# Reordering the first three weight blocks of a hybrid SSM/convolution layer: product 6 ahead of product 7, a table setup that starts later, and its small copies on VectorE

## The chip, the cores and the metric

The kernel runs on one core of a Trainium2 chip. The metric is the device time of one execution in microseconds (us). The kernel before takes 1282.01 us, the median of three runs (1280.66, 1282.01 and 1284.53).

The core has a matrix engine (TensorE, PE in the profile), VectorE (DVE), ScalarE (ACT), GpSimd (POOL) and SyncE (SP), which here only issues DMAs. Each engine works off its own list of instructions in the order in which the program wrote them; semaphores make it wait for another engine's result.

## The reference, cut to what matters

```python
proj = x @ w_in + b_in                         # x: 1024 x 1024, w_in: 1024 x 4096
u, h, c_gate, b_gate, gate_a, gate_b = split(proj)
y_a = s5_ssm(u, lambda, log_dt, B, C, D)       # complex diagonal scan, 32 groups of 64 states
g   = gelu(y_a)
y_a = (g * sigmoid(g @ glu_w + glu_b)) @ w_ssm_out
y_b = (b_gate * causal_conv(c_gate * h)) @ w_conv_out
mix = (sigmoid(gate_a) * y_a + sigmoid(gate_b) * y_b) @ w_o
x   = layer_norm(alpha * x + mix)
x   = layer_norm(alpha * x + (silu(x @ w_gate) * (x @ w_up)) @ w_down)
```

All of it is in float32. The part that the change touches is the first projection (blocks of `w_in`), the constants of the scan, which are worked out on the chip from `lambda` and `log_dt`, and the order of the first blocks of `w_gate` and `w_up`.

## The kernel before, in words

**Products.** A pair of weight columns blocks times the 1024 tokens is a 2 x 2 by 2 x 2 block product, done in seven products in Strassen's way. `WOP` (L152) and `XOP` (L154) say which sum or difference of blocks each of the seven products m = 1 to 7 takes on the weight side and on the x side. Each operand of a product is split into a high and a low float32r part ("lo" and "hi"): ScalarE writes the rounded high part (L121, or L137 and L138 when the rounded copy also goes to a PSUM tile `hp`), VectorE subtracts it from the operand (L115). A product is then 12 matmuls of 128x512: four slices k of the contraction, each lo·hi, hi·lo and hi·hi (L183 to L185). In the first stage the products 2 and 5 of the first three pairs skip the split and use unsplit float32 operands (L179).

**PSUM banks.** `BANK_OF` (L157) puts products 2 and 4 of a pair in its bank 0, 5 and 3 in bank 1, 1 and 7 in bank 2, 6 in bank 3. Product 7 is accumulated on top of product 1, so it can only start after ScalarE has copied product 1 out of the bank (the tile `ec`, or `z` for the second pair, L237). A bank of a later product takes the PSUM buffer of an earlier one: six buffers go round in order of allocation. `Pair.ev` (L207 to L263) is run after each product and issues the combinations: copies `ea`, `eb`, `ec` on ScalarE, `ea+eb` and `ec-ea` on GpSimd (L239, L241), `b0-ea`, `b1+ec` and the last additions on VectorE (L253, L255, L257, L259), then the epilogue of the block.

**Steps.** A step is one product of one pair. `LEAD` (L305, L306) is the order of the first 21 steps: three pairs interleaved, first products 2, 4, 5, 3 of each, then 1, 7, 6 of pairs 0 and 1, then 1, 7, 6 of pair 2. In the first projection the pairs are u0, u2 and gt0 (tiles `_u`, `_u`, `_gt`); in the gated feed-forward stage they are f0, f1, f2 (`_f`). `run` (L325) issues the instructions of step s in this order: its own loads, the weight sum of step s+4 (GpSimd, tile `t`, or `ws` for the unsplit products), the weight split of step s+3 (ScalarE and VectorE, tiles `wh` and `wl`), one turn of each background generator that is due, the matmuls of step s, epilogues that are due, the `mid` work, and then `Pair.ev`.

**The x operands.** `make_x` (L432) makes the x operands of the first stage in `mid` of steps 0 to 19: for products 4, 3, 1, 7, 6 a sum on GpSimd in four slices (tile `xs`, L449) and two slices later the split (tiles `xh`, `xl`); for 5 and 2 the split alone. The sums use two tiles in turn.

**The setup of the SSM branch.** `setup` (L497) is a generator that works out the tables `E`, `Lim`, `nLre`, `Mre`, `sMim` and `ph8` from the parameters. It is a chain of small VectorE operations, 128x32 to 128x288, in 22 pieces (each ends at a `yield`), with two Sin activations on ScalarE. Pieces 1 to 11 are issued ahead of step 0 (L1349, L1375, L1379, L1387); from step 0 on one piece is issued per step, ahead of the matmuls of the step (L1391): 12 at step 0, 13 at step 1, the Sin piece 16 at step 4, the piece that writes `Mre` at step 10, the piece that writes `sMim` at step 13. After that it idles until step 21, closes its scratch and starts the branch's own generators. `Mre` and `sMim` are each written by eight small instructions on GpSimd, one per power j (L627, L634).

**The feed-forward stage.** The same `LEAD` orders the first 21 steps there. The third pair's banks 0 and 1 are copied out early to tiles `keep` (L242 to L247), which the first projection doesn't do.

Of the kernel before, what the change touches and what calls it, by code (L numbers as in the profile page):

```python
# [47 lines left out]
def kernel(  # L48
# [22 lines left out]
    V, S, G, PE = nc.vector, nc.scalar, nc.gpsimd, nc.tensor  # L71
# [27 lines left out]
    sgn = const.tile([P, 3], F32, tag="sgn", name="sgn")  # L99
# [5 lines left out]
    def tt(o, a, b, op, eng=V):  # L105
        eng.tensor_tensor(o, a, b, op)  # L106
# [10 lines left out]
    def ts(o, a, s1, s2, op0, op1, eng=V):  # L117
        eng.tensor_scalar(o, a, s1, s2, op0, op1)  # L118
# [184 lines left out]
    steps = []  # L303
    ORD_A = (2, 5, 1, 4, 3, 7, 6)
    LEAD = [(i, m) for m in (2, 4, 5, 3) for i in (0, 1, 2)]  # L305
    LEAD += [(i, m) for m in (1, 7, 6) for i in (0, 1)] + [(2, 1), (2, 7), (2, 6)]  # L306

    def add_pairs(pairs, lead, nl):
        for i, m in lead:
            steps.append(pairs[i].step(m))  # L310
        for p in pairs[nl:]:
            base = len(steps)
            for m in ORD_A:
                steps.append(p.step(m))
            for i, back in ((1, 7), (0, 6)):
                steps[base - back].pre.append(lambda p=p, i=i: p.load(i))
# [27 lines left out]
    def start(gen, s=0):  # L344
        bg.append([gen, s])
# [63 lines left out]
    def mkpair(f0, f1, nm, ep, f):  # L409
        p = Pair(w1[f0], w1[f1], nm, xcombo, ep)  # L410
        p.f = f
        return p

    gp_ = [mkpair(16 + d, 24 + d, f"gt{d}", epi_g, d) for d in range(8)]
    pairs = [mkpair(0, 1, "u0", epi_u, 0), mkpair(2, 3, "u2", epi_u, 2), gp_.pop(0)]
# [16 lines left out]
    def make_x():  # L432
        waiting = []

        def low(h, l, k, src):
            (psplit if k % 2 else split)(h[:, k], l[:, k], src)

        for n, m in enumerate((4, 3, 1, 7, 6, 5, 2)):
            op = XOP[m]
            if len(op) == 3:  # L440
                sums = xcp.tile([P, 4, 512], F32, tag=("xh2", "xl2")[n % 2], name=f"xs{m}")
            h = xh[m] = xcp.tile([P, 4, 512], F32R, tag=f"xh{m}", name=f"xh{m}")
            l = xl[m] = xcp.tile([P, 4, 512], F32R, tag=f"xl{m}", name=f"xl{m}")
            for k in range(4):
                if len(op) == 1:
                    src = xr[op[0]][:, k]
                else:
                    src = sums[:, k]
                    tt(src, xr[op[1]][:, k], xr[op[2]][:, k], OPS[op[0]], G)  # L449
                waiting.append((h, l, k, src))  # L450
                if len(waiting) > 2:
                    low(*waiting.pop(0))
                yield 1
        for w in waiting:
            low(*w)
            yield 1
# [17 lines left out]
    for p in pairs[:3]:  # L474
        p.drops = {4: 1}
        p.whole = {2: wsum, 5: wsum}
    add_pairs(pairs, LEAD, 3)
    for n, i, q in ((1, 1, 0), (3, 0, 1), (5, 1, 1)):
        steps[n].pre.append(lambda i=i, q=q: pairs[i].load(q))
    steps[7].pre.append(lambda: load_f(pairs[2], 1))  # L480
# [16 lines left out]
    def setup():  # L497
# [3 lines left out]
        Mre = tb["Mre"] = pre.tile([P, NG, 8], F32, tag="Mre", name="Mre")  # L501
        sMim = tb["sMim"] = pre.tile([P, NG, 8], F32, tag="sMim", name="sMim")
# [8 lines left out]
        def carve(*shape, at=None):  # L511
            n = int(np.prod(shape))
            o = used[0] if at is None else at
            if at is None:
                used[0] += n
            t = scr[:, o : o + n]
            return t.rearrange("p (a b) -> p a b", a=shape[0]) if len(shape) == 2 else t
# [11 lines left out]
        m, r, q = carve(NG), carve(NG), carve(NG)  # L529
# [92 lines left out]
        x8, y8 = t9[:, :, 0:8], u9[:, :, 0:8]  # L622
# [1 line left out]
        mul(y8, Lim[:, :, 0:8], fib)  # L624
        sub(x8, x8, y8)
        for j in range(8):
            G.tensor_copy(Mre[:, :, j], x8[:, :, 7 - j])  # L627
        yield 1
        mul(x8, nLre[:, :, 0:8], fib)
        mul(y8, Lim[:, :, 0:8], frb)  # L630
        add(x8, x8, y8)
        yield 2
        for j in range(8):
            G.tensor_scalar_mul(sMim[:, :, j], x8[:, :, 7 - j], sgn[:, 0:1])  # L634
        ts(nLre, nLre, sgn[:, 0:1], -1.0, ALU.mult, ALU.mult)
        while psum_state["n"] > 4 or next(xg, None):
            yield 1
# [604 lines left out]
    fps = []  # L1242
# [7 lines left out]
    fps[2].kept = lambda i: cst_["zp"].tile([P, 512], F32, tag=f"keep{i}", name=f"keep{i}")  # L1250
    for p in fps[:3]:
        p.drops = {4: 1}
    add_pairs(fps, LEAD, 3)
    n_end = len(steps)
    def begin_d0():
        flush()
# [89 lines left out]
    ramp = tb["ramp"] = pre.tile([P, P], F32, tag="ramp", name="ramp")  # L1346
    dss = tb["dss"] = pre.tile([16, NG], F32, tag="dss", name="dss")
    early_setup = setup()
    next(early_setup)  # L1349
    raw = pairs[0].raw[1] = wring.tile([P, KT, P], F32, tag="raw", name="raw_u0_1", bufs=4)  # L1350
# [32 lines left out]
    steps[2].add()  # L1383
    steps[2].split()
    steps[3].add()
    for _ in range(4):
        next(early_setup)  # L1387
    xg = make_x()
    for n, cnt in enumerate((2, 2, 2, 1, 2, 1, 2, 1, 2, 1, 2, 1, 2, 2, 1, 2, 1, 1, 1, 1)):
        steps[n].mid.append(lambda cnt=cnt: [next(xg, None) for _ in range(cnt)])  # L1390
    start(early_setup)  # L1391

    def spin():
        for it in list(bg):
# [143 lines left out]
    for n in range(len(seq)):  # L1538
        m, kp = seq[n]
# [156 lines left out]
```

## Time and profile before

| what | value |
|---|---|
| median of three runs | 1282.01 us (1280.66 to 1284.53) |
| profiled execution, its own time | 1284.58 us |
| profiled execution, span from first to last instruction | 1282.8 us |
| granted TensorE clock, mean | 0.979 |
| TensorE busy | 1208.3 us, 94% of the span |
| VectorE busy | 830.6 us, 65% |
| GpSimd busy | 792.8 us, 62% |
| ScalarE busy | 763.8 us, 60% |

In a row of the timeline the columns are: start in us, duration in us, engine, line, operation, output<-inputs, shape, number of instructions merged into the row, and in square brackets the idle time before it on its engine and what ended it. In the table of waits a row reads: engine, tile and line of the waiting instruction, what it waited for, us in total, number of waits, the longest. In the table by stretches each engine's busy us stands with its number of instructions, in the order PE, PE weight loads, DVE, ACT, POOL, then the granted clock, the DMA share and GB/s.

### The profile page before, as it was taken

To read this page: it belongs to the slowest core of one execution; us is meant where nothing else is said; L and a number is where in the kernel's file an instruction comes from. 1 tells how busy PE (TensorE), PEld (TensorE's weight loads), DVE (VectorE), ACT (ScalarE), POOL (GpSimd) and SP (SyncE) were. 2 spreads that over 40 slices of the span, in tenths; PEclk is the share of its full clock that TensorE was granted. 3 is DMA by queue.
4 is the path that set the end of the run, shared out by engine and by line. 5 is a ranking of instruction groups with operands and counts; after the bars stand their busy time and mean duration, and the time that the engine had idled before them with its cause. 6 is when DMAs were issued, how large, how long until landed. Compare 5 with 4: busy or idle time off the path is not lost. (4 is left out here: it accounts for less than half of the span.)

```text
span 1282.8 us, 16767 instructions
## 1 busy us (share of the span) xinstructions
PE 1208.3 (94%) x5341; PEld 977.2 (76%) x5341; DVE 830.6 (65%) x1322; ACT 763.8 (60%) x1359; POOL 792.8 (62%) x609
## 2 busy tenths in 40 slices
PE   4968999999998999999988999999999999999996
PEld 1646787777777888888866888888888887888776
DVE  8784787979754757588875444434444437667777
ACT  2765777787886424133574555545555545778891
POOL 4575888788753213322488877787787774544466
PEclk8988999999999999999989999999999999999999
DMA  7213244344357535323502533232233426936312
GB/s 252 66 66 99 66 125 120 103 143 138 112 161 224 188 123 183 128 89 116 173 33 94 177 108 114 93 123 99 83 115 107 140 91 247 379 98 214 106 43 90
DMA packets 88455, 167.63 MB, mean 131 GB/s; under 512 B 17840, under 2 KB 27056, under 8 KB 88112
## 3 DMA queue, kind: packets, MB, share of 16 engines
q1 hardware_dynamic: 87760, 166.44, 38.9%
q8 instruction: 42, 0.69, 0.2%
q14 instruction: 45, 0.37, 0.1%
q10 hardware_dynamic: 608, 0.13, 0.1%
HBM read 116.34 MB, written 44.83 MB: 126 GB/s over the span
## 5 line engine op out<-in xcount | busy, mean ns | idle before, releaser
L183 PE MATMUL ps_f<-x1h,wl_f 128*128 128x512 f32 x616 | 242.1, 393 | 8.4 <-ACT keep L246 2.3
L184 PE MATMUL ps_f<-x1l,wh_f 128*128 128x512 f32 x616 | 240.9, 391 | 0.6 <-DVE x1l L115 0.6
L185 PE MATMUL ps_f<-x1h,wh_f 128*128 128x512 f32 x616 | 241.1, 391 | 0.0
L115 DVE TENSOR_TENSOR wl_f<-t_f,hp 128x512 fp32r<-128x512 f32 x107 | 73.5, 687 | 168.9 <-ACT hp L137 168.6
L137 ACT ACTIVATE hp<-t_f 128x512 fp32r<-128x512 f32 x107 | 64.4, 602 | 175.8 <-POOL t_f L106 169.3
L183 PEld LDWEIGHTS ps_f<-x1h,wl_f 128*128 128x128 f32 x616 | 116.4, 189 | 35.4 <-ACT keep L246 2.7
L184 PEld LDWEIGHTS ps_f<-x1l,wh_f 128*128 128x128 f32 x616 | 116.5, 189 | 24.8 <-DVE x1l L115 1.0
L185 PEld LDWEIGHTS ps_f<-x1h,wh_f 128*128 128x128 f32 x616 | 116.3, 189 | 24.4
L106 POOL TENSOR_TENSOR tB<-B,B 128x512 f32<-128x512 f32 x55 | 71.3, 1297 | 84.1 <-DVE rBl L115 45.3
L1517 PE MATMUL pe<-rBh,rAl 128*128 128x512 f32 x297 | 116.1, 391 | 2.5 <-DVE acc L112 1.6
L1518 PE MATMUL pe<-rBl,rAh 128*128 128x512 f32 x297 | 116.0, 390 | 1.2 <-DVE rBl L115 1.2
L1519 PE MATMUL pe<-rBh,rAh 128*128 128x512 f32 x297 | 115.6, 389 | 0.0
L183 PE MATMUL ps_gt<-xh,wl_gt 128*128 128x512 f32 x216 | 88.7, 411 | 12.0 <-ACT ec_gt L237 7.2
L185 PE MATMUL ps_gt<-xh,wh_gt 128*128 128x512 f32 x216 | 86.5, 401 | 0.0
L184 PE MATMUL ps_gt<-xl,wh_gt 128*128 128x512 f32 x216 | 86.1, 399 | 0.0
L106 POOL TENSOR_TENSOR t_f<-raw_f,raw_f 128x512 f32<-128x512 f32 x63 | 81.8, 1298 | 2.2 <-DVE wl_f L115 2.2
L1517 PEld LDWEIGHTS pe<-rBh,rAl 128*128 128x128 f32 x297 | 55.7, 188 | 16.3 <-DVE acc L112 2.5
L1518 PEld LDWEIGHTS pe<-rBl,rAh 128*128 128x128 f32 x297 | 55.7, 188 | 13.7 <-DVE rBl L115 2.3
L138 ACT ACTIVATE wh_f<-t_f 128x512 fp32r<-128x512 f32 x107 | 66.0, 617 | 0.0
L1519 PEld LDWEIGHTS pe<-rBh,rAh 128*128 128x128 f32 x297 | 55.7, 188 | 11.5
L106 POOL TENSOR_TENSOR t_f<-raw_f 128x512 f32<-128x512 f32 x43 | 56.5, 1323 | 10.1 <-DMA raw_f<-in_wgu 9.5
L109 POOL TENSOR_TENSOR hid<-sgf,ec_f 128x512 f32<-128x512 f32 x21 | 27.5, 1310 | 55.9 <-DVE sgf L109 31.7
(410 smaller groups left out, 3260.6 us busy)
## 6 DMA issues: line engine op xcount, KB each, us to landing
raw_f<-in_wgu SPq DMA_DIRECT2D x45, 512.0 KB, 4.1
As<-a_d SPq DMA_DIRECT2D x77, 256.0 KB, 3.7
a_d<-hs SPq DMA_DIRECT2D x55, 256.0 KB, 2.0
B<-in_wd SPq DMA_DIRECT2D x44, 256.0 KB, 5.0
s_d<-sg SPq DMA_DIRECT2D x32, 256.0 KB, 2.6
sgd<-s_d SPq DMA_DIRECT2D x16, 512.0 KB, 3.4
raw_gt<-in_w SPq DMA_DIRECT2D x15, 512.0 KB, 4.7
a_d<-hid SPq DMA_DIRECT2D x22, 256.0 KB, 2.1
```

Source lines behind the costliest of these rows:

```text
L106: eng.tensor_tensor(o, a, b, op)
L109: eng.tensor_tensor(o, a, b, ALU.mult)
L115: eng.tensor_tensor(o, a, b, ALU.subtract)
L137: S.activation(hp, raw, AF.Copy)
L138: S.activation(hi, raw, AF.Copy)
L183: PE.matmul(ps, self.lo[:, k, :], xh[:, k, :], start=first and k == 0, stop=False, skip_group_check=True)
L184: PE.matmul(ps, self.hi[:, k, :], xl[:, k, :], start=False, stop=False, skip_group_check=True)
L185: PE.matmul(ps, self.hi[:, k, :], xh[:, k, :], start=False, stop=last and k == 3, skip_group_check=True)
L1517: PE.matmul(ps, al[:, c], bh, start=kp == 0, stop=False)
L1518: PE.matmul(ps, ah[:, c], bl, start=False, stop=False)
L1519: PE.matmul(ps, ah[:, c], bh, start=False, stop=kp == NK - 1)
```

## The change

It has three parts, and the result is computed by the same formulas as before.

1. The order of the lead. In the first projection product 6 comes ahead of product 7 for all three pairs (`LEAD_A`), and `make_x` makes the operand of product 6 ahead of that of 7. In the feed-forward stage (`LEAD_D`) only the third pair has 6 ahead of 7; its order of x operands stays.
2. The setup. Ahead of step 0 only piece 8 is issued in the place where pieces 8 to 11 were; piece 9 follows at step 4, and from there one piece per step, so that the Sin piece 16 is at step 11, piece 18 at step 13, piece 19 at step 16, the piece with `Mre` at step 17, piece 21 at step 18 and the piece with `sMim` at step 20. What comes at step 21 stays there.
3. The sixteen small instructions that write `Mre` and `sMim` are issued on VectorE and not on GpSimd.

```diff
     ORD_A = (2, 5, 1, 4, 3, 7, 6)
     LEAD = [(i, m) for m in (2, 4, 5, 3) for i in (0, 1, 2)]
-    LEAD += [(i, m) for m in (1, 7, 6) for i in (0, 1)] + [(2, 1), (2, 7), (2, 6)]
+    LEAD_A = LEAD + [(i, m) for m in (1, 6, 7) for i in (0, 1)] + [(2, 1), (2, 6), (2, 7)]
+    LEAD_D = LEAD + [(i, m) for m in (1, 7, 6) for i in (0, 1)] + [(2, 1), (2, 6), (2, 7)]
...
-        for n, m in enumerate((4, 3, 1, 7, 6, 5, 2)):
+        for n, m in enumerate((4, 3, 1, 6, 7, 5, 2)):
...
-    add_pairs(pairs, LEAD, 3)
+    add_pairs(pairs, LEAD_A, 3)
...
         for j in range(8):
-            G.tensor_copy(Mre[:, :, j], x8[:, :, 7 - j])
+            V.tensor_copy(Mre[:, :, j], x8[:, :, 7 - j])
...
         for j in range(8):
-            G.tensor_scalar_mul(sMim[:, :, j], x8[:, :, 7 - j], sgn[:, 0:1])
+            V.tensor_scalar_mul(sMim[:, :, j], x8[:, :, 7 - j], sgn[:, 0:1])
...
-    add_pairs(fps, LEAD, 3)
+    add_pairs(fps, LEAD_D, 3)
...
     steps[3].add()
-    for _ in range(4):
-        next(early_setup)
+    next(early_setup)
     xg = make_x()
...
-    start(early_setup)
+    start(early_setup, 4)
```

## The prediction

> **What bounds the kernel now.** I read the page first, then the table by stretches, then the waits of TensorE in the first 112 us, then the timeline of each engine there.
>
> ```profile
> span 1282.8 us, 16767 instructions
> 20.00:40.00 20.00, 8.15 (x21) 5.82 (x22) 19.48 (x29) 7.33 (x12) 12.70 (x11) 0.66 0.35 108
> 160.00:200.00 40.00, 40.00 (x204) 33.23 (x204) 33.79 (x49) 30.04 (x51) 33.58 (x26) 1.00 0.40 119
> 760.00:1200.00 440.00, 439.09 (x1933) 362.18 (x1932) 228.53 (x346) 270.65 (x501) 294.61 (x232) 1.00 0.42 146
> ```
>
> From 160 us on TensorE has no idle time to speak of (440 of 440 us, at full clock), and its order of work is fixed. So whatever the change does to the time at which TensorE finishes the leads goes nearly undiminished to the end. In 20 to 40 us it is the other way round: TensorE works 8 of 20 us, VectorE 19.5. These are the waits of TensorE up to 112 us:
>
> ```profile
> PE ps_u L184 <- DVE xl L115: 8.8, 1, 8.8
> PE ps_u L183 <- ACT ec_u L237: 7.3, 1, 7.3
> PE ps_gt L183 <- ACT ec_gt L237: 6.8, 1, 6.8
> PE ps_u L183 <- DVE scr L112: 3.5, 1, 3.5
> ```
>
> They sum to 26.4 us. The first and the last are step 3, which stands behind the setup on VectorE; the two `ec` waits are product 7 of pair 0 and of pair gt0, which may not be added to product 1 before ScalarE has copied that out. The same places in TensorE's timeline:
>
> ```profile
> 15.91 3.60 PE L179 MATMUL ps_gt<-xr,ws 128*128 128x512 f32 x8
> 43.46 7.03 PE L179 MATMUL ps_u<-xr,ws 128*128 128x512 f32 x16
> 53.35 0.79 PE L183 MATMUL ps_u<-xh,wl_u 128*128 128x512 f32 x1
> 62.44 0.50 PE L183 MATMUL ps_u<-xh,wl_u 128*128 128x512 f32 x1 [0.26 <-DVE wl_u L115]
> 77.60 0.80 PE L183 MATMUL ps_u<-xh,wl_u 128*128 128x512 f32 x1 [7.33 <-ACT ec_u L237]
> 78.62 0.63 PE L185 MATMUL ps_u<-xh,wh_u 128*128 128x512 f32 x1
> 79.05 0.63 PE L183 MATMUL ps_u<-xh,wl_u 128*128 128x512 f32 x1
> 83.09 0.40 PE L184 MATMUL ps_u<-xl,wh_u 128*128 128x512 f32 x1
> 83.32 0.39 PE L185 MATMUL ps_u<-xh,wh_u 128*128 128x512 f32 x1
> 100.80 0.80 PE L183 MATMUL ps_gt<-xh,wl_gt 128*128 128x512 f32 x1 [6.78 <-ACT ec_gt L237]
> 110.08 0.50 PE L183 MATMUL ps_hc<-xh,wl_hc 128*128 128x512 f32 x1 [0.78 <-DVE ec_gt L112]
> ```
>
> Row 15.91 is step 2, 43.46 begins step 6, 53.35 step 9, 62.44 step 12, 77.60 step 14, 100.80 step 19, 110.08 step 21. After the wait of 7.33 us the starts lie 0.43 us apart (78.62, 79.05), later 0.23 us (83.09, 83.32): a step of twelve matmuls takes 12 x 0.23 = 2.75 us, and the one behind a long wait 12 x 0.20 = 2.4 us more. A long wait that goes saves this too, a new one costs it.
>
> **Part 1: the setup leaves the front.**
>
> ```profile
> 13.71 2.64 DVE L115 TENSOR_TENSOR scr<-scr 128x32 f32<-128x32 f32 x3
> 30.37 1.81 DVE L115 TENSOR_TENSOR xl<-xs,xh 128x512 fp32r<-128x512 f32 x1
> L115 DVE TENSOR_TENSOR xl<-xs,xh 128x512 fp32r<-128x512 f32 x10 | 12.9, 1295 | 0.4 <-ACT xh L121 0.4
> L115 DVE TENSOR_TENSOR xl<-xs,hp 128x512 fp32r<-128x512 f32 x10 | 6.8, 678 | 1.1 <-ACT hp L137 1.1
> L560 DVE COPY E<-scr 128x32 f32<-128x32 f32 x1 | 0.2, 190 | 0.0
> 16.36 1.25 DVE L569 TENSOR_SCALAR scr<-scr 128x32 f32<-128x32 f32 x1
> 67.11 0.42 DVE L109 TENSOR_TENSOR scr<-nLre,scr 128x256 f32<-128x256 f32 x1
> 70.34 1.46 DVE L109 TENSOR_TENSOR scr<-nLre,scr 128x256 f32<-128x256 f32 x1 [0.22 <-POOL Mre L627]
> 15.04 5.00 POOL L106 TENSOR_TENSOR xs<-xr,xr 128x512 f32<-128x512 f32 x4 [0.17 <-DMA xr<-in_xT]
> 24.26 2.50 POOL L106 TENSOR_TENSOR xs<-xr,xr 128x512 f32<-128x512 f32 x2 [3.00 <-DMA xr<-in_xT]
> ```
>
> By L497 to L587, 22 operations of pieces 9 to 13 and two weight splits lie between the rows 13.71 and 30.37; two more of piece 9 come just before. So (16.7 - 2 x 0.6) / 22 = 0.7 us each, although an operation of this size takes 0.19 alone (L560). The rows show why: the same 128x256 product takes 0.42 us at 67.11, where GpSimd is idle, and 1.46 at 70.34, where it runs; L569 takes 1.25 us beside GpSimd's 1.25 us sums (5.00 / 4); the subtraction with both operands in SBUF takes 1.295, the one whose high part `hp` is in PSUM 0.678.
>
> Without pieces 9 to 13 the split of x for step 3 follows GpSimd's sums directly: the fourth is ready at 20.04, two ScalarE passes and the VectorE subtraction end it at about 22.7, and the last three matmuls of step 3 at 23.4. Steps 4 and 5 take 2 x 2.75, to 28.9, where before they ended at 43.46: a lead of 14.5 us. Steps 6 to 8 keep their length (53.35 - 43.46 = 9.9), so step 9 could start at 39. Nothing in DMA forbids it: the last x quarter, by row 24.26, is there before product 3 wants it.
>
> The pieces are not gone. They now run in steps 4 to 8, and VectorE has to pass, from the x sums of product 3 (26 us) to the weights of step 12: 24 of these operations, five subtractions at 1.3 and four at 0.6, four weight splits at 0.6, three combinations at 0.6, which is 13.1 us and 24 x s. I take s = 0.5, between 0.19 and 0.7, because GpSimd, which no longer sums continuously there, leaves gaps while it waits for the copy `eb` of step 6 and for the ring of two `t` tiles. That is 26 + 13.1 + 12 + about 2.5 of waiting = 53.7 for the start of step 12, against 62.44: the lead has shrunk to **8.7 us** (13 at s = 0.3, 4 at s = 0.7). What is late in steps 10 and 11 is the weights' low part behind the pieces.
>
> The Sin piece moves behind the first Sigmoid of gt0 in ScalarE's order, which adds a table load:
>
> ```profile
> 46.22 1.28 ACT L406 ACT_TABLE_LOAD   x1
> ```
>
> That is 0 to 1.3 us; I take nothing, since ScalarE waits for VectorE there; without this cover it would delay the x split of product 7 by 1.3. Queued behind the Sin are that split, the Sigmoid of gt0 and the weights of step 15. Pieces 9 to 22 issue no DMA, so SP's queue is unaffected.
>
> **Part 2: 6 ahead of 7, first projection.**
>
> ```profile
> 78.61 1.74 POOL L115 TENSOR_TENSOR ec_u<-ec_u,ea_u 128x512 f32<-128x512 f32 x1
> 102.16 0.69 DVE L112 TENSOR_TENSOR ec_gt<-ps_gt,ec_gt 128x512 f32<-128x512 f32 x1 [1.18 <-POOL ec_gt L115]
> 68.39 1.92 POOL L627 COPY Mre<-scr 128x32 f32<-128x32 f32 x8 [3.57 <-DVE scr L115]
> 81.56 3.56 POOL L634 TENSOR_SCALAR sMim<-scr,sgn 128x32 f32<-128x32 f32 x8
> ```
>
> Step 14 is now (0, 6), which has a bank of its own and needs no copy: the 7.33 us and the 2.4 of slow clock go. GpSimd also loses 3.57 us of standing still, 1.92 and 3.56 us of work, which lay ahead of the `ec` subtraction. But (1, 6) in step 15 takes the PSUM buffer of pair 0's bank 1, whose last reader is the addition L255, behind the copy, GpSimd's subtraction (1.3 to 1.74) and VectorE (0.69). Ordering the queues by hand with the durations above: step 13 starts at 57.7 behind piece 14 (three operations of up to 1.25) and a split, step 14 at 62.5 behind piece 15 (four operations, 3.0) and two x subtractions, and TensorE is done with it at 65.2. ScalarE comes to the copy of pair 0 at 68.8, behind the Sin, the Sigmoid, the weights of step 15 and three x splits; copy, subtraction and addition end at 71.3. A wait of 6 us comes back one step later, with its slow clock: step 15 ends at 76.3 (71.3 + 2.75 + 2.4), steps 16, 17 and 18 (2.75 each) at 84.6 instead of 94.0 (100.80 - 6.78); the lead is **9.4 us**.
>
> The third pair is worse placed: (2, 6) follows (2, 1) directly and takes the buffer of gt0's bank 1, so it waits for copy, subtraction and addition, where (2, 7) waited only for the copy: 102.85 against 100.80, 2 us longer at before's pace. And VectorE's addition now stands behind pieces 19, 20 and 21.
>
> **Part 3: copies on VectorE.** Ahead of that addition lie 8 + 3 + 8 + 3 = 22 setup operations. Before's trace has no such copy on VectorE beside GpSimd: 0.19 alone is the lower end, 1.46 by the row 70.34 the upper. GpSimd has here only a weight sum per step, 1.25 of some 3.5 us, so I take 0.35, nearer to the lower end: 7.7 us. From the weights of step 18 (78.2, right behind those of step 17) VectorE then passes five x subtractions and three combinations (5.3 in all), three weight splits (1.8), these 7.7 and the addition itself (0.6), and ends that at about 93.4. Step 19 waits 8.8 us (93.4 - 84.6; 6.78 before), and with slow clock steps 19 and 20 end near 101.2. The eight `sMim` copies (0.19 each or more) stand ahead of the closing addition, after which the banks are reopened: 2 us. Step 21 starts at about 103, against 110.08: **7 us earlier**.
>
> [...]
>
> **Part 4: feed-forward stage.**
>
> ```profile
> 665.28 0.58 ACT L246 ACTIVATE keep<-ps_f 128x512 f32<-128x512 f32 x1
> 687.66 0.59 ACT L237 ACTIVATE ec_f<-ps_f 128x512 f32<-128x512 f32 x1
> 688.30 0.50 PE L183 MATMUL ps_f<-x1h,wl_f 128*128 128x512 f32 x1 [1.90 <-ACT ec_f L237]
> ```
>
> Here bank 1 of the third pair was copied to `keep` at 665.28, so (2, 6) finds its buffer free, and by the time of (2, 7) `ec` is copied (688.25). The 1.90 us go: **1.9 us**. If the buffer were not free, nothing would be gained.
>
> **Sum.** 7 + 1.9 = 8.9 us off the profiled execution's 1284.58 (span 1282.8 and 1.8 around it) gives 1275.7. The median of the runs lies 2.57 lower, so the forecast is 1282.0 - 8.9 = **1273**. About 0.3% (3.8 us) is what a measurement of this kernel can tell from no change.
>
> **The rivals.**
>
> *The front's lead stays.* VectorE's pieces find GpSimd mostly idle and cost 0.2 in both places; the 14.5 us of step 5 arrive at step 21, and 1.9 more: 1282 - 16.4 = 1266. For it: both engines then stretch each other less. Against: GpSimd's sums for products 3 and 1 run back to back there.
>
> *The lead is eaten at step 19.* Every part up to step 18 comes true, but the addition that frees gt0's bank is late by 6 us more (0.6 per setup operation): 7 - 6 + 1.9 = 3, 1279, no measurable change.
>
> *Slower: VectorE becomes the bound of steps 16 to 20.* If the 22 operations ahead of the addition at L255 take about 1.0 us each, it comes 14 us later than I took: 7 - 14 + 1.9 = -5, 1287. It decides from 0.35 + 8.9 / 22 = 0.75 us each. For it: 1.25 and 1.46 in the rows, and GpSimd's instructions are lengthened too (1.74 at 78.61). Against: GpSimd works about a third of the time in those steps. At 1.46 each it would be 1297.
>
> *The change does not act as described in the lead:* if the first wait were due to the x transfer and not to VectorE, the front would gain little; row 24.26 speaks against it, and I fold it into the third case.
>
> **How the numbers follow.** Forecast (1268 to 1278) 0.47, the lead stays 0.24, eaten 0.17, slower 0.12. Faster by over 0.3% (below 1278.2): 0.70, from the first two less the edge of the forecast; within 0.3%: 0.18; slower: 0.12. The range 1260 to 1284 takes in the first three cases, s between 0.2 and 0.7 among them; the forecast's own is 1268 to 1278.
>
> **What would show it.** Right: no wait of TensorE near 23 to 32 us, step 9 near 39, step 12 near 54, step 14 without `ec`, a wait in step 15 or 19 that ends with the addition at L255, step 21 near 103, and no 1.9 us wait in the feed-forward lead. Wrong: step 12 still after 60 us (pieces as dear as before), `Mre` and `sMim` copies above 0.75 us each on VectorE, or step 21 at 110 or later.

## The result, and the profile after

The changed kernel takes 1275.58 us, the median of five runs (1273.34 to 1276.85), against 1282.19 (1280.66 to 1284.53) for the kernel before in five. The ratio is 0.9943 with a 95% interval from 0.9926 to 0.9959: 6.6 us faster, where 8.9 were forecast. The profiled execution took 1276.85 us (1284.58 before), and its span is 7.7 us shorter. First the page's head and the table by stretches of the changed kernel (columns as in the prediction):

```profile
span 1275.1 us, 16761 instructions
...
20.00:40.00 20.00, 18.34 (x58) 10.53 (x58) 15.89 (x23) 11.42 (x20) 14.26 (x12) 1.00 0.54 181
...
760.00:1200.00 440.00, 438.18 (x1931) 361.87 (x1930) 231.65 (x351) 275.03 (x511) 289.11 (x227) 1.00 0.43 146
```

In 20 to 40 us TensorE now works 18.3 of 20 us instead of 8.2, and VectorE 15.9 instead of 19.5. In 760 to 1200 us TensorE is busy all the time, as before (438.2 and 439.1 of 440 us). The changed kernel's waits of TensorE in the first 112 us:

```profile
PE ps_gt L183 <- DVE scr L112: 6.1, 1, 6.1
PE ps_gt L183 <- ACT ec_gt L237: 5.8, 1, 5.8
...
PE ps_u L183 <- DVE ec_u L112: 4.3, 1, 4.3
PE ps_u L183 <- DVE wl_u L115: 2.4, 1, 2.4
...
PE ps_u L184 <- DVE xl L115: 0.4, 1, 0.4
```

The 8.8 us of step 3 have become 0.4, the 3.5 us at its start are gone, and product 7 of pair 0 no longer waits 7.3 us for its copy. In their place stand a new wait of 6.1 us, one of 4.3 and one of 2.4. The same places in TensorE's timeline, the starts of steps 6, 9, 11, 12, 14, 15, 19, 20 and 21:

```profile
27.65 7.03 PE L179 MATMUL ps_u<-xr,ws 128*128 128x512 f32 x16
...
39.32 0.50 PE L183 MATMUL ps_u<-xh,wl_u 128*128 128x512 f32 x1 [1.22 <-ACT eb_u L234]
...
51.50 0.77 PE L183 MATMUL ps_gt<-xh,wl_gt 128*128 128x512 f32 x1 [6.08 <-DVE scr L112]
...
56.19 0.39 PE L183 MATMUL ps_u<-xh,wl_u 128*128 128x512 f32 x1
...
64.38 0.50 PE L183 MATMUL ps_u<-xh,wl_u 128*128 128x512 f32 x1 [2.43 <-DVE wl_u L115]
...
73.01 0.80 PE L183 MATMUL ps_u<-xh,wl_u 128*128 128x512 f32 x1 [4.28 <-DVE ec_u L112]
...
85.49 0.39 PE L183 MATMUL ps_gt<-xh,wl_gt 128*128 128x512 f32 x1
...
94.16 0.79 PE L183 MATMUL ps_gt<-xh,wl_gt 128*128 128x512 f32 x1 [5.77 <-ACT ec_gt L237]
...
99.45 0.60 PE L183 MATMUL ps_hc<-xh,wl_hc 128*128 128x512 f32 x1
```

Against before's starts of 43.46, 53.35, 77.60 and 110.08 for steps 6, 9, 14 and 21, the lead is 15.8, 14.0, 13.2 and 10.6 us. The wait at step 11 eats part of the first lead. VectorE's timeline of the changed kernel shows what it is:

```profile
42.19 3.81 DVE L112 TENSOR_TENSOR scr<-scr 128x32 f32<-128x32 f32 x3
46.03 1.17 DVE L118 TENSOR_SCALAR scr<-scr 128x32 f32<-128x32 f32 x1
47.24 1.20 DVE L115 TENSOR_TENSOR scr<-scr 128x32 f32<-128x32 f32 x1
48.36 1.79 DVE L115 TENSOR_TENSOR xl<-xs,xh 128x512 fp32r<-128x512 f32 x1
...
50.68 0.67 DVE L115 TENSOR_TENSOR wl_gt<-xz,hp 128x512 fp32r<-128x512 f32 x1
51.27 0.63 DVE L112 TENSOR_TENSOR scr<-scr 128x32 f32<-128x32 f32 x3
...
90.30 0.87 DVE L628 COPY Mre<-scr 128x32 f32<-128x32 f32 x8
...
98.85 1.35 DVE L635 TENSOR_SCALAR sMim<-scr,sgn 128x32 f32<-128x32 f32 x8
```

Five operations of piece 12 take 6.2 us beside GpSimd's sums (1.26 to 1.30 us each). The weights of step 11 (50.68) stand behind them, and TensorE starts 0.15 us after these are done. The list names `scr L112` (51.27), VectorE's last instruction to begin before that start, and a different one from what TensorE needed: the operands of step 11 are the ones in row 50.68. The sixteen copies, on the other hand, cost VectorE 0.11 and 0.17 us each.

### The profile page after: what moved, and what is told of

Read it like the earlier page. It is cut to its first block, busy times and chain, and to the rows that moved or that the text cites. A ratio compares the mean times of both kernels' runs of the same rounds, so it can differ in the third digit from the quotient of the medians.

```text
span 1275.1 us, 16761 instructions
## 1 busy us (share of the span) xinstructions
PE 1207.8 (95%) x5341; PEld 976.8 (77%) x5341; DVE 836.1 (66%) x1338; ACT 765.7 (60%) x1360; POOL 787.9 (62%) x593
## 5 line engine op out<-in xcount | busy, mean ns | idle before, releaser
L183 PE MATMUL ps_f<-x1h,wl_f 128*128 128x512 f32 x616 | 241.7, 392 | 8.7 <-ACT keep L246 3.9
L183 PEld LDWEIGHTS ps_f<-x1h,wl_f 128*128 128x128 f32 x616 | 116.2, 189 | 35.7 <-ACT keep L246 4.3
L183 PE MATMUL ps_gt<-xh,wl_gt 128*128 128x512 f32 x216 | 89.3, 413 | 19.1 <-ACT ec_gt L237 6.2
L183 PEld LDWEIGHTS ps_gt<-xh,wl_gt 128*128 128x128 f32 x216 | 42.1, 195 | 32.0 <-issue 7.1
```

Source lines behind the costliest of these rows:

```text
L183: PE.matmul(ps, self.lo[:, k, :], xh[:, k, :], start=first and k == 0, stop=False, skip_group_check=True)
```

## The experiments

Each was timed beside the kernel before on the same chip, and its ratio is to those runs. Each edit is against the changed kernel. "The first `pk` matmul" is the first matmul of the branch's own matrices, the mark at which the front is over: it starts at 127.2 us before and at 116.7 after. Two more traces of the same front, of the changed kernel once more and of the run with the feed-forward order undone, have it at 117.0 and 117.9, so a difference of about 1 us at this mark says little. The trace of the kernel before is of an execution 2.4 us above its median (1284.58 against 1282.19), so some of a lead measured against it may be that execution's own.

### One part undone at a time

**The setup back in front of step 0.**

```diff
-    next(early_setup)
+    for _ in range(4):
+        next(early_setup)
...
-    start(early_setup, 4)
+    start(early_setup)
```

> The changed kernel with the setup put back to the front (pieces 8 to 11 ahead of step 0, then one per step from step 0); orders and copies stay changed. My theory: the 12 us that TensorE stood behind the setup at step 3 come back, step 9 starts near 53 us instead of 39, and since nothing later made up for it, step 21 starts 5 to 8 us later than in the changed kernel (99.5): the time is 1280 to 1284, about that of before. Rival, the lead of the front is eaten anyway: the pieces cost VectorE the same wherever they stand, the end of the lead is set by VectorE's total work and by the ec waits, and the time stays at 1275 to 1277.

Measured: 1281.13 us, ratio 0.999 (0.998 to 1.0). Nearly the whole gain is gone, as the theory has it; the first `pk` matmul starts at 121.5. In its waits of TensorE up to 121 us stands the wait for `xl` again:

```profile
PE ps_u L184 <- DVE xl L115: 7.4, 2, 6.2
...
```

**The old order in the first projection** (`LEAD_A` and `make_x`).

```diff
-    LEAD_A = LEAD + [(i, m) for m in (1, 6, 7) for i in (0, 1)] + [(2, 1), (2, 6), (2, 7)]
+    LEAD_A = LEAD + [(i, m) for m in (1, 7, 6) for i in (0, 1)] + [(2, 1), (2, 7), (2, 6)]
...
-        for n, m in enumerate((4, 3, 1, 6, 7, 5, 2)):
+        for n, m in enumerate((4, 3, 1, 7, 6, 5, 2)):
```

> The changed kernel with product 7 ahead of 6 again in the first projection (lead and x operands); the setup, the copies and the order of the feed-forward stage stay changed. My theory: the wait of product 7 of pair 0 for the ec copy comes back in step 14, and is worth 3 us more than the wait for the PSUM buffer that stands in its place now (4.3 us); the third pair's wait moves from step 20 to 19 and stays as long: 1278 to 1281. Rival, one wait replaces the other: the ec copy is late for the same reason as the addition behind it, so the order is worth under 1.5 us: 1274 to 1277.

Measured: 1277.42 us, ratio 0.997 (0.9959 to 0.9982), and the first `pk` matmul at 120.5. Its timeline of TensorE has both `ec` waits, each longer than before, because the setup's lead arrives at them:

```profile
71.87 0.79 PE L183 MATMUL ps_u<-xh,wl_u 128*128 128x512 f32 x1 [8.48 <-ACT ec_u L237]
...
95.18 0.80 PE L183 MATMUL ps_gt<-xh,wl_gt 128*128 128x512 f32 x1 [7.99 <-ACT ec_gt L237]
```

So the order is worth some 2 us once the setup has moved (1.8 by the medians, between theory and rival; the two intervals just touch at 0.9959): without it part of the setup's lead is spent waiting for copies.

**The table copies back on GpSimd.**

```diff
-            V.tensor_copy(Mre[:, :, j], x8[:, :, 7 - j])
+            G.tensor_copy(Mre[:, :, j], x8[:, :, 7 - j])
...
-            V.tensor_scalar_mul(sMim[:, :, j], x8[:, :, 7 - j], sgn[:, 0:1])
+            G.tensor_scalar_mul(sMim[:, :, j], x8[:, :, 7 - j], sgn[:, 0:1])
```

> The changed kernel with the sixteen table copies on GpSimd again. My theory: on VectorE they cost 0.9 us (Mre) and 1.4 us (sMim); on GpSimd they hold up the ec subtraction and the weight sums behind them for the wait on piece 20 plus 1.9 us, and sMim 3.6 us ahead of the first weight sums of the next pairs: 1277 to 1280. Rival, they lie beside idle time: GpSimd works only a third of the time in steps 16 to 20, and the end is set by the ec copy on ScalarE: 1274 to 1276.5.

Measured: 1274.57 us, ratio 0.9949 (0.9936 to 0.9963): no difference from the changed kernel that these runs can tell. My theory that the copies on VectorE were worth something fell, and the rival holds. GpSimd does the `Mre` copies in 0.24 us each and the `sMim` ones in 0.44 (3.56 us for eight in the kernel before), at a place where nobody is seen to wait for them.

**The old order of the third pair in the feed-forward stage.**

```diff
-    LEAD_D = LEAD + [(i, m) for m in (1, 7, 6) for i in (0, 1)] + [(2, 1), (2, 6), (2, 7)]
+    LEAD_D = LEAD + [(i, m) for m in (1, 7, 6) for i in (0, 1)] + [(2, 1), (2, 7), (2, 6)]
```

> The changed kernel with product 7 ahead of 6 again for the third pair of the feed-forward stage only. My theory from the trace: the 1.9 us wait for ec that went came back three steps later as waits of 1.3 and 0.3 us, since ScalarE's epilogue stands behind a DMA out of a staging tile; so this order is worth nothing: 1274.5 to 1276.5. Rival, the forecast's step: it is worth 1.9 us: 1277 to 1278.

Measured: 1277.28 us, ratio 0.9975 (0.9963 to 0.9986), 1.7 us over the changed kernel by the medians, so "nothing" is not borne out. The traces say less. From the first to the last start of the stage's lo·hi matmuls (L183 on `ps_f`) it is 433.3 us before (622.5 to 1055.8) and 434.1 in this run (614.3 to 1048.4), the two with the old order. With the new order it is 432.8 after (614.7 to 1047.5), 432.6 to 432.9 in ten other runs of this document, and 434.1 in one (613.9 to 1048.0, the pieces in the hole of step 3). So the stage itself gains 0.5 to 1.3 us by the new order, and one execution with it shows no gain.

### The changed kernel again, and three attempts to go further

**The changed kernel once more**, with no edit, beside the next three.

> The changed kernel itself once more, beside the others of this set on one chip. Both theories: 1274 to 1277, with TensorE's waits of 6.1 us at step 11, 4.3 at step 15 and 5.8 at step 20.

Measured: 1275.43 us, ratio 0.9948 (0.9936 to 0.996).

**Pieces 9 to 11 in the hole of step 3**, where VectorE waits for ScalarE and GpSimd for x.

```diff
+    steps[3].pre.append(lambda: [next(early_setup) for _ in range(3)])
     start(early_setup, 4)
```

> The changed kernel with pieces 9 to 11 of the setup issued at the start of step 3, so that VectorE does them between about 21.4 and 25.3 us, where it and GpSimd both stand still for the x quarter; piece 12 then comes at step 4 and so on. My theory (the pieces are dear only beside GpSimd's sums, and what is left of the front's lead is lost to that): the 14 operations cost 0.2 to 0.3 us each there instead of 10 us between 26 and 39; the wait at step 11 (6.1 us and its slow clock) goes, step 12 starts before 52 us instead of 56.5, and 3 to 6 us of it reach the end: 1270 to 1273. Rival, the ec waits set the end of the lead: step 12 comes earlier, but the waits of steps 15 and 20 grow by as much: 1274.5 to 1277.

Measured: 1278.05 us, ratio 0.9968 (0.9956 to 0.998). The moved pieces are cheap there: their 128x32 operations take 0.17 to 0.21 us, though three of the four 128x128 ones take 1.2 to 1.3. But the next pieces meet GpSimd's sums instead (three additions from 29.55 us on take 1.23 each, beside a run of five sums from 30.71), and step 11 waits as long, now for another copy:

```profile
PE ps_gt L183 <- ACT eb_gt L234: 7.4, 1, 7.4
```

The edit also brings the Sin piece from step 11 to step 8, ahead of that copy in ScalarE's order. ScalarE waits 4.50 us with the Sin, until VectorE has finished piece 15 at 49.4 us, and the copy starts at 53.57, against 43.95 in the changed kernel. My expectation of a gain fell, but what the cheaper pieces alone are worth this run does not tell.

**Product 1 of the third pair ahead of the sevens.**

```diff
-    LEAD_A = LEAD + [(i, m) for m in (1, 6, 7) for i in (0, 1)] + [(2, 1), (2, 6), (2, 7)]
+    LEAD_A = LEAD + [(0, 1), (1, 1), (0, 6), (1, 6), (2, 1), (0, 7), (1, 7), (2, 6), (2, 7)]
```

> The changed kernel with product 1 of the third pair of the first projection three steps earlier (after product 6 of pair 1, ahead of the sevens), so that its copy out of the bank has four steps before product 7 wants it. My theory: the wait of step 20 (5.8 us) and its slow clock (2.4) go, the wait for the buffer at step 15 stays: step 21 at 91 to 94 instead of 99.5, and 4 to 7 us at the end: 1269 to 1272. Rival, VectorE's queue is what is late there, not the place of the copy: the closing additions still come at 98 to 100 us, the wait turns up at step 21 where the banks are opened anew: 1274.5 to 1277.

Measured: 1277.76 us, ratio 0.9965 (0.9952 to 0.9979). The wait of 5.8 us at step 20 is gone and step 21 starts 5.6 us earlier than in the changed kernel. By the first `pk` matmul nothing of it is left (117.9, where the changed front has 116.7 to 117.9). Its timeline of TensorE from step 21 on, the rows with the longer waits:

```profile
93.82 0.50 PE L183 MATMUL ps_hc<-xh,wl_hc 128*128 128x512 f32 x1 [1.44 <-DVE wl_hc L115]
...
98.92 0.79 PE L183 MATMUL ps_hc<-xh,wl_hc 128*128 128x512 f32 x1 [1.65 <-ACT xh L138]
...
117.86 0.39 PE L696 MATMUL pk<-cp,bst 128*16 128x128 f32 x2 [1.41 <-DVE cp L115]
```

TensorE now runs into weights and x parts that are not split yet. The rival holds: taking TensorE's wait away does not bring VectorE's queue forward. The last two closing additions of gt0 start at 98.95 and 101.69 us, where they start at 97.65 and 100.38 in the changed kernel.

**Both of these.** The edits are the last two together.

> The two edits together: pieces 9 to 11 at step 3 and product 1 of the third pair three steps earlier. If both causes are as I have it, they add: 1264 to 1269. If VectorE's total work sets the end of the lead, not more than the better of the two: 1270 to 1276.

Measured: 1277.43 us, ratio 0.9966 (0.9954 to 0.9979). They don't add.

### Is VectorE the bound? More work on it, and less

**25 operations more in steps 4 to 8**, in two kinds. Their results are used by nobody; `dmy` is scratch that stands free there, filled once ahead of step 0. The diff is of the kind with two inputs; the other has `V.bn_stats(dmy[:, 2, 0:6], dmy[:, 0])` in its place.

```diff
...
+    dmy = tb["dmy"]
+
+    def more():
+        for _ in range(5):
+            V.tensor_tensor(dmy[:, 2], dmy[:, 0], dmy[:, 1], ALU.mult)
+
+    for n in range(4, 9):
+        steps[n].pre.append(more)
     start(early_setup, 4)
```

> The changed kernel with five more VectorE operations of 128x32 at each of steps 4 to 8 (25 in all), each with two inputs in SBUF, as the setup's own sums and products; their results are used by nobody. This prices VectorE's time in the stretch to which the change moves the setup. Theory (VectorE's queue is the bound there): at about 0.7 us each, as the 24 moved operations took, 17 us more of VectorE's time; VectorE's idle time of 18.5 us takes some of it, and 5 to 10 us reach the end: 1281 to 1286. Rival (slack at steps 12 to 20 takes it all): within 1.5 us of 1275.5.

> As the run before, but each of the 25 added operations is a bn_stats of 128x32, with one input in SBUF. Theory (the price is the two inputs beside a GpSimd sum, not the number of operations): each 0.2 us or less, 5 us in all, and 0 to 2 us at the end: 1275.5 to 1277.5. Rival (any small operation queued between the sums costs its wait): near the run before, 1280 or more.

Measured: two inputs, 1283.14 us, ratio 1.0004 (0.9993 to 1.0014), all of the change's gain gone; one input, 1276.86, ratio 0.9965 (0.9952 to 0.9977), 1.3 us over the changed kernel by the medians. First VectorE's timeline with two inputs, the same five operations at two places, then the tile view's row of one kernel and of the other (ns, shortest, median and longest):

```profile
26.93 6.19 DVE L1397 TENSOR_TENSOR scr<-scr 128x32 f32<-128x32 f32 x5
...
40.53 1.09 DVE L1397 TENSOR_TENSOR scr<-scr 128x32 f32<-128x32 f32 x5
```
```profile
L1397 DVE TENSOR_TENSOR scr<-scr x25: 182/193/1316, 26.9 to 58.0; 128x32 f32<-128x32 f32 x25
```
```profile
L1397 DVE BATCH_NORM_STATS2 scr<-scr x25: 177/195/196, 27.3 to 51.3; 128x6 f32<-128x32 f32 x25
```

The median is the same; of these two kinds only the one with two inputs is ever stretched: its longest is 1316 ns, where the longest of one input is 196. 1316 ns is about one GpSimd sum (1.27 us at 27.49 in the changed kernel). The number of inputs is not all that matters: the setup's own one-input TENSOR_SCALAR of 128x32 took 1.17 us in row 46.03 above. `bn_stats` also writes only 6 columns, and which of its properties spares it is not shown.

The front of four kernels in the table by stretches, from 13 us to the first `pk` matmul: before, after, two inputs more, and pieces 9 to 13 on GpSimd, which is told next.

```profile
13.00:127.20 114.20, 84.93 (x296) 59.96 (x294) 84.24 (x123) 63.31 (x113) 74.49 (x70) 0.85 0.33 107
```
```profile
13.00:116.70 103.70, 83.43 (x294) 59.04 (x292) 85.25 (x139) 64.54 (x113) 67.17 (x52) 0.90 0.33 111
```
```profile
13.00:123.90 110.90, 85.03 (x296) 59.30 (x294) 91.40 (x164) 64.39 (x112) 66.83 (x52) 0.89 0.31 104
```
```profile
13.00:119.70 106.70, 83.52 (x295) 58.63 (x293) 68.58 (x114) 64.15 (x112) 75.34 (x77) 0.92 0.33 107
```

The third busy number is VectorE's. The change did not make it work less (84.2 before, 85.3 after): the front became shorter because VectorE's idle time in it fell from 30.0 to 18.5 us. The two other traces of the same front have 83.0 and 84.7 us of work and 21.0 and 20.2 of idle time, which shows how far these numbers scatter. With two inputs more, VectorE is busy 6.2 us longer and the front is 7.2 longer, nearly one for one. The 25 operations themselves took 15.1 us (25 x 603 ns), but the setup's own operations behind them became cheaper (four subtractions went from 1195 to 443 ns on average), as if each sum of GpSimd stretched whichever of these operations met it. With one input more VectorE is busy 0.3 us longer (85.55) and the front lasts 1.5 longer (105.20), hardly more than the scatter.

**Pieces 9 to 13 on GpSimd instead of VectorE**, and the same with the third-pair order (the `LEAD_A` edit above; it puts product 1 of the third pair ahead of the sevens, not of product 6). All their operations change engine; the one fused operation among them becomes two.

```diff
-        mul(th, li, dt)
-        V.tensor_scalar_mul(hl, th, 4097.0)
-        sub(hh, hl, th)
+        mul(th, li, dt, G)
+        G.tensor_scalar_mul(hl, th, 4097.0)
+        sub(hh, hl, th, G)
...
-        V.scalar_tensor_tensor(pr[:, 3], hh, C3, pr[:, 3], ALU.mult, ALU.add)
+        G.tensor_scalar_mul(tm[:, 3], hh, C3)
+        add(pr[:, 3], tm[:, 3], pr[:, 3], G)
...
```

> Setup pieces 9 to 13 (24 small operations, one of them now split in two) are computed on GpSimd instead of VectorE; all else as changed. Theory (VectorE's queue is what the front runs on, and those pieces cost it about 17 us between 26 and 52 us): without them the first `pk` matmul comes 4 to 7 us sooner than 116.7, the wait at step 11 is gone, and the time is 1269 to 1272 us. Rival (VectorE's time in steps 4 to 8 is hidden, the buffers of the closing copies set the end): the first `pk` matmul stays within 1 us of 116.7 and the time is 1274.5 to 1277. A third way: GpSimd, which makes the sums of the input and weight pieces, becomes late itself, and the same waits come back behind it: 1277 or more.

> As the run before, and product 1's third pair is taken ahead of product 6 for both first products of the lead, as in the earlier run with that order. Theory: with VectorE early, its addition of that pair's third part is done sooner and the wait at step 20 stays away too, so both gains add: 1266 to 1270 us. Rival: the order is worth nothing, whatever VectorE does, and the time is that of the run before within 1.5 us.

Measured: 1278.95 us, ratio 0.998 (0.997 to 0.999), and 1279.96, ratio 0.9988 (0.9977 to 0.9999): slower than the changed kernel, the third way. VectorE does lose 16.7 us of work (85.25 to 68.58), yet the front gets 3.0 longer. VectorE's waits between 13 and 119 us, in the first of these two kernels, show why:

```profile
...
DVE eb_u L106 <- POOL ea_u L112: 4.8, 1, 4.8
DVE eb_gt L106 <- POOL ea_gt L112: 4.7, 1, 4.7
```

In the changed kernel the wait for `ea_u` is 0.6 us and that for `ea_gt` is not among its longer ones. GpSimd's combinations and sums now stand behind the pieces (it works almost without a gap from 23.8 to 62.9 us), and VectorE waits for them. TensorE's wait at step 11 is gone, but four waits for `wl_u` weights, 10.3 us in all, stand in its list, where the changed kernel has one of 2.4.

## Why the prediction was right, and where it was not

The forecast came true in its sign and its first cause. The sizes were off in both directions and partly cancelled: the lead at step 21 was 3.6 us larger than worked out (10.6 against 7), and 2.8 us of it were lost further on, where the sum lost nothing. That 1275.58 us came so near to 1273 is partly luck.

**Step 3 and the first lead: right.** The wait was VectorE's setup and not a transfer; step 6 started at 27.65 (28.9 was worked out) and step 9 at 39.32 (39). Undoing the setup's move alone brings the wait back and takes 5.6 of the 6.6 us. (The four waits listed in the prediction are not all up to 112 us: the list also has 5.1 us at the very start and three entries of 0.6 to 2.0.)

**The price of 24 moved operations: too low.** I took s = 0.5 us, with GpSimd leaving gaps. From 26 to 52 us their rows add up to about 17 us, 0.7 each: as much as in the old place. GpSimd's sums of the x operands had moved forward with them: a run of four that began at 35.93 us before is one of five from 29.95. Step 12 started at 56.2 and its lead was 6.2 us, not 8.7. "What is late in steps 10 and 11 is the weights' low part behind the pieces" is what step 11 shows; step 10 has no wait.

**Steps 14 to 18: the starts right within 2 us.** The wait of 7.3 us at step 14 is gone, a shorter one (2.4) for weights stands there, and the wait comes back at step 15 behind the addition (72.26 + 0.69), 4.3 us instead of 6. Step 15 could start at 73.01; 71.3 was worked out. Most of that difference is, by the order of ScalarE's queue, the table load that the sum put at nothing. The load for the Sin is covered as argued, but the one back to the Sigmoid is not: from 65.17 us on ScalarE works without a gap, and the copy of pair 0 comes at 70.28 instead of 68.8.

```profile
65.80 1.28 ACT L407 ACT_TABLE_LOAD   x1
...
70.28 0.58 ACT L237 ACTIVATE ec_u<-ps_u 128x512 f32<-128x512 f32 x1
```

**Step 19: the step that failed.** That (2, 6) takes the buffer of gt0's bank 1, "so it waits for copy, subtraction and addition", was wrong. Step 19 starts at 85.49, right behind step 18, and has no wait in it, while that addition comes at 95.85:

```profile
95.85 0.69 DVE L112 TENSOR_TENSOR ec_gt<-ps_gt,ec_gt 128x512 f32<-128x512 f32 x1 [1.17 <-POOL ec_gt L115]
```

A step that starts 10 us ahead of it cannot need it, so (2, 6) got another buffer. The six buffers therefore do not simply go round in order of allocation, as I had described them ahead of the prediction. Which one it got the trace does not show; by the order of VectorE's queue, bank 3 of pair 0 and of pair 1 had been read for the last time by the additions at 78.80 and 82.59 us (0.68 each) and were free by then. The wait stands at step 20 instead, for the copy alone. ScalarE's timeline of the changed kernel has that copy behind an epilogue that waits for VectorE:

```profile
92.39 0.72 ACT L359 ACTIVATE us<-z_u,b1s 128x512 f32<-128x512 f32 x1 [2.03 <-DVE z_u L112]
93.02 0.61 ACT L121 ACTIVATE xh<-xr 128x512 fp32r<-128x512 f32 x1
93.53 0.58 ACT L237 ACTIVATE ec_gt<-ps_gt 128x512 f32<-128x512 f32 x1
```

**Part 3: the size was right, its meaning was not.** For the 22 operations I took 7.7 us; their rows give 7.0, with the copies at 0.11 and 0.17 each, below the lower end of my range. The case "slower" needed 0.75 each. But with the copies on GpSimd the time is the same, so by these runs this part neither gives nor costs anything that can be measured.

**Step 21: 99.45, not 103.** The addition did not hold up step 19, and the 2 us for the closing were not paid: there is no wait at step 21. The lead there is 10.6 us and not 7.

**"Nearly undiminished": wrong.** From a lead of 10.5 at the first `pk` matmul 7.8 are left at the first matmul of `w_o` (527.9 before, 520.1 after). In the 13 other traces of this document, of the changed kernel and its variants, the lead over before shrinks between that mark and the first matmul of the feed-forward stage (622.5 before) by 1.0 to 4.5 us, but for two, where it stays or grows by 0.4; with the setup back in front it is 5.7 at the mark and 3.2 there. Two stretches between corresponding `pk` matmuls show where it goes, before and after:

```profile
127.22:149.03 21.81, 21.81 (x105) 17.70 (x105) 17.55 (x29) 18.16 (x31) 17.66 (x14) 1.00 0.23 64
211.36:253.26 41.90, 38.15 (x181) 30.65 (x180) 35.14 (x49) 31.80 (x57) 33.72 (x25) 1.00 0.33 91
```
```profile
116.71:140.26 23.55, 22.26 (x105) 17.65 (x105) 17.49 (x29) 18.20 (x31) 19.39 (x16) 1.00 0.29 80
202.59:247.01 44.42, 39.73 (x181) 31.80 (x180) 37.66 (x52) 32.57 (x58) 34.83 (x26) 0.96 0.33 92
```

The same matmuls take 1.7 us longer in the first stretch, which now has a wait for `cp` (1.05 us, on VectorE) where before had none. They take 2.5 longer in the second, where a wait for `ec_hc` grew from 1.23 to 2.18 us and the clock fell to 0.96; later stretches give some back. I had read 40 busy us in 160 to 200 as the rule for all that follows; there are waits in 200 to 350 us, and one of them grew with the lead.

**Part 4: open in size.** 1.9 us were forecast, the medians show 1.7, the traces 0.5 to 1.3 in the stage itself. The 1.90 us wait for `ec_f` is gone; waits of 1.3 for `ea_f` and 0.3 for `wh_f` stand in the lead instead.

**What bounds the front after the change.** That added VectorE time reaches the end nearly one for one is shown, and so is that the lead gained for TensorE at step 20 is lost again behind splits that VectorE and ScalarE have not done yet. That VectorE is the only bound is not: the one run that took work off it put that on GpSimd, and GpSimd became late. Less work on both was not tried. None of the variants beats the changed kernel beyond its interval.

## What to carry to other kernels

Look for the stretch in which the busiest engine isn't TensorE and ask how long that engine idles there: here the gain was VectorE's idle time (30.0 us before, 18.5 to 21.0 after), not its work. A wait removed further down is worth only what the next operand's maker is ahead, so read that engine's queue before counting the wait as a gain. A lead gained early shrinks at every later place that waits for something else; count those waits over the whole run, not in one good stretch.

## What the hardware showed that I had not expected

The 25 added operations cost VectorE less than their own time: they took 15.1 us, but VectorE's busy time in the front grew by 6.2, with as many GpSimd instructions there (52) as without them. When the 25 operations were put in, the setup's four 128x32 subtractions in 20 to 60 us went from 1195 to 443 ns on average, as these groups of the changed kernel and of the one with two inputs more show:

```profile
L115 DVE TENSOR_TENSOR scr<-scr 128x32 f32<-128x32 f32 x4 | 4.8, 1195 | 0.1
```
```profile
L115 DVE TENSOR_TENSOR scr<-scr 128x32 f32<-128x32 f32 x4 | 1.8, 443 | 0.1
```

The slow clock did not begin where the wait ended, and once it did not come at all. After the 2.43 us wait at 64.38 the first matmuls of the step start 0.23 us apart, and only from 65.96 on 0.43, in the changed kernel's timeline:

```profile
65.19 0.39 PE L183 MATMUL ps_u<-xh,wl_u 128*128 128x512 f32 x1
65.42 0.39 PE L184 MATMUL ps_u<-xl,wh_u 128*128 128x512 f32 x1
65.65 0.52 PE L185 MATMUL ps_u<-xh,wh_u 128*128 128x512 f32 x1
65.96 0.63 PE L183 MATMUL ps_u<-xh,wl_u 128*128 128x512 f32 x1
66.39 0.63 PE L184 MATMUL ps_u<-xl,wh_u 128*128 128x512 f32 x1
```

The granted clock is 0.50 from there to 68.50. In the repeat of the changed kernel the same step also waits 2.43 us, and its slow starts begin 0.6 us after the wait (65.53 less 64.94). In the run with the feed-forward order undone it waits 2.31 us, and no slow start follows within the step. So the onset differs between executions of the same work (here 1.6 us, 65.96 less 64.38), and no trace here shows what sets it.
